# Linear attention in a hybrid decoder step: level products for each head alone, on 64 rows, into two banks

## The chip, the cores and the metric

The kernel runs on one core of one Trainium2 chip. A core has a matrix engine (TensorE, PE in the profile, with its weight loads shown apart as PEld), VectorE (DVE), ScalarE (ACT), GpSimd (POOL) and a queue engine for transfers (SyncE, SP). Operands lie in SBUF, 128 partitions ("rows") wide. TensorE writes its results to PSUM, which has eight banks of 512 fp32 columns. Each engine runs its own instructions in order and waits for others through semaphores.

The metric is device time in microseconds (us) for the whole program. Before the change it is 1334.49 us, the median of three runs (1328.85 to 1334.85).

## The reference, cut to what matters

One layer of a decoder: a norm, one input projection, eight heads of windowed attention beside four heads of gated linear attention, and an output projection. The prompt has 2048 positions, and a sample batch has 64 more. Only the linear attention is touched by the change. Its heads have 64 key columns and 128 value columns. `log_a` is the logarithm of the forget gate, per position and key column:

```python
log_a = jax.nn.log_sigmoid((g_lr @ w_gate_up + b_gate)) / GATE_TAU      # GATE_TAU = 16

def step(state, xs):                     # one chunk of positions
    qc, kc, vc, gc = xs
    b = jnp.cumsum(gc, axis=2)
    diff = b[:, :, :, None, :] - b[:, :, None, :, :]
    decay = jnp.exp(jnp.where(causal[:, :, None], diff, -jnp.inf))
    scores = jnp.einsum('bhtk,bhsk,bhtsk->bhts', qc, kc, decay)
    o = (jnp.einsum('bhts,bhsv->bhtv', scores, vc)
         + jnp.einsum('bhtk,bhkv->bhtv', qc * jnp.exp(b), state))
    b_last = b[:, :, -1]
    state = (jnp.exp(b_last)[..., None] * state
             + jnp.einsum('bhsk,bhsv->bhkv', kc * jnp.exp(b_last[:, :, None] - b), vc))
    return state, o
```

The score of a query `t` and a key `s` needs a decay that depends on both and on the key column, so it isn't one matrix product. It becomes one for a block of queries against a block of keys before them, if both are scaled relative to one position between the blocks: `q_t k_s exp(b_t - b_s) = (q_t exp(b_t - b_m)) (k_s exp(b_m - b_s))`.

## The kernel before

**Levels.** The kernel uses chunks of 128 positions and splits the triangle of a chunk into levels (`LEVELS`, block sizes B = 1, 2, 4, 8, 16, 32, 64). On level B the positions fall into pairs of neighbouring blocks of B. The queries of each second block meet the keys of the first block, both scaled relative to the last position of the first block. The seven levels and the diagonal cover every pair of positions once.

**Units.** `gla_core` treats 256 positions, so two chunks and four heads; there are eight such units for the prompt (tiles named `..._e`). Two heads lie together on the 128 rows: head 2p on rows 0 to 63 and head 2p+1 on rows 64 to 127. So kT, qT and the summed gates b have two halves p of 256 columns. For each level there is a front and a back:

- `front` (lines 229 to 255). GpSimd subtracts the reference position from b (tile `D`, line 236). ScalarE takes exponentials of it into `E` (line 244): one for the keys on all 128 rows, and two for the queries, each on the 64 rows of one head, into two separate layers of `E`. The rest of these two layers is zero from the start. VectorE multiplies keys by layer 0 (`ks`, line 249), and queries by layers 1 and 2 at once (`qbd`, line 252). So `qbd` has the queries twice: once with zeros in place of the second head, once with zeros in place of the first.
- `back` (lines 257 to 292). TensorE multiplies `ks` (128 rows, 64 columns, the stationary operand) with both layers of `qbd`. Because of the zeros, one product over 128 rows gives the scores of each of the two heads. Below B = 64 (line 281) a product has 64 keys and 2 x 32 queries, eight products a level, alternating between output rows 0 to 63 and 64 to 127. VectorE copies the valid ones under a mask into `Ac` (line 287). At B = 64 (line 267) it has 64 keys and 2 x 64 queries, four products a level, and ScalarE copies the result into `full` (line 273). An fp32 product is two instructions on TensorE, each with its weight load.

**PSUM.** The level scores take tiles of the pool `ps_S`, which has two banks in turn: a level's products may start as soon as the copy of the level before last is done. Attention's scores (`qk`, line 436) and the transposes of the mix (line 1611) take tiles of the same pool, at other times.

**What follows.** When all levels of a unit are in, `filled` moves the triangle into `full`, and `chunk` (line 1266) multiplies each head's scores with the values (line 1289), adds the state's part (line 1283), and updates the state `Sbd` (lines 1275 and 1296).

**Order.** `gla_prompt` runs front of level s, then back of level s - 2, then yields; it is woven with the projections (`project`, line 1127, which keep TensorE busy with f16 products `acc_g`, `acc_vb`, `acc_gb`) and with `late_dots` (line 1515 on GpSimd, line 970 on VectorE) by fixed shares. The framework's planner then places instructions on each engine's queue by a simulated timeline, and adds semaphores where a tile, or in PSUM a bank, is written or read by another engine.

Of the kernel before, what the change touches and what calls it, by code (L numbers as in the profile page):

```python
# [7 lines left out]
F32 = mybir.dt.float32  # L8
# [10 lines left out]
P = 128  # L19
# [33 lines left out]
def tile_hymba(ctx: ExitStack, tc: tile.TileContext, A: dict):  # L53
# [86 lines left out]
        DVE.scalar_tensor_tensor(out, a[:n], 1.5, r[:n], ALU.add, ALU.mult)  # L140


    class gla_core:

        def __init__(self, pools, st, row0, n, C, levels, scan_m, mask, tagp, full=None, keep=None):
# [17 lines left out]
        def turn(self):  # L163
# [10 lines left out]
            Ac = self.Ac = keep.tile(  # L174
                [P, nch * 4, 64], F32, name=f"Ac_{tagp}", tag="A", bufs=two
            )
            POOL.tensor_tensor(
                Ac[:C],
                ident64[:C].unsqueeze(1).to_broadcast([C, nch * 4, 64]),
                dd[:C].unsqueeze(2).to_broadcast([C, nch * 4, 64]),  # L180
                ALU.mult,
            )

# [45 lines left out]
        def front(self, li):  # L229
            gt, st, n, B = self.pools[1], self.st, self.n, self.levels[li]  # L230
            halves = lambda f: f.rearrange("p (m two B) -> p m two B", two=2, B=B)
            M = n // B
            bv = halves(self.b[:].rearrange("p a c -> p (a c)"))
            D = gt.tile([P, 2 * n], F32, name=f"D_{self.tagp}_{B}", tag="D", bufs=2)
            dv = halves(D[:])
            dec = POOL.tensor_tensor(  # L236
                dv, bv, bv[:, :, 0:1, B - 1 : B].to_broadcast([P, M, 2, B]), ALU.subtract
            )
            E = st["E"][li % 2]
            ev = E[:, :, :n].rearrange("p i (m B) -> p i m B", B=B)  # L240
            for i, (rows, half) in enumerate(
                ((slice(0, P), 0), (slice(0, 64), 1), (slice(64, P), 1))
            ):
                ACT.activation(  # L244
                    ev[rows, i], dv[rows, :, half, :], AF.Exp, scale=(2 * half - 1) / 16.0
                )
            ks, qbd = st["ks"][li % 3], st["qbd"][li % 3]
            kv, qv = (halves(f.rearrange("p a c -> p (a c)")) for f in (self.kT, self.qT))
            DVE.tensor_tensor(  # L249
                halves(ks[:, : 2 * n])[:, :, 0, :], kv[:, :, 0, :], ev[:, 0], ALU.mult  # L250
            )
            que = DVE.tensor_tensor(  # L252
                qbd[:, :, :n].rearrange("p i (m B) -> p i m B", B=B),
                qv[:, :, 1, :].unsqueeze(1).to_broadcast([P, 2, M, B]), ev[:, 1:3], ALU.mult,
            )
            st["pins"] = (dec.ins, que.ins)

        def back(self, li):
            st, n, C, nch, B = self.st, self.n, self.C, self.nch, self.levels[li]
            ps_s, Ac = self.pools[3], self.Ac  # L260
            ks, qbd = st["ks"][li % 3], st["qbd"][li % 3]
            sc = ps_s.tile([P, 512], F32, name=f"sc_{self.tagp}_{B}", tag="S")
            if B == 64:

                for c in range(nch):
                    for p in range(2):
                        PE.matmul(
                            sc[:64, (c * 2 + p) * P : (c * 2 + p + 1) * P],
                            ks[:, p * n + c * C : p * n + c * C + 64],
                            qbd[:, :, (p * nch + c) * 64 : (p * nch + c + 1) * 64],  # L270
                            start=True, stop=True,
                        )
                ACT.activation(
                    self.full[0:64, :, 64:], sc[:64].rearrange("p (g t) -> p g t", t=64), AF.Copy
                )
                return
            for c in range(nch):
                for p in range(2):
                    o = (c * 2 + p) * 64
                    for k0 in range(0, C, 64):  # L280
                        PE.matmul(
                            sc[k0 : k0 + 64, o : o + 64],
                            ks[:, p * n + c * C + k0 : p * n + c * C + k0 + 64],
                            qbd[:, :, p * (n // 2) + (c * C + k0) // 2 :][:, :, :32],
                            start=True, stop=True,
                        )
            DVE.copy_predicated(
                Ac[:C].rearrange("p g (m two B) -> p g m two B", two=2, B=B)[:, :, :, 1, :],
                self.mask[:C, li].bitcast(I32).unsqueeze(1)
                .to_broadcast([C, nch * 4, 32]).rearrange("p g (m B) -> p g m B", B=B),  # L290
                sc[:C, : nch * 128].rearrange("p (g m B) -> p g m B", g=nch * 4, B=B),
            )

        def queries(self):
# [85 lines left out]


    with ExitStack() as c1:
        ps_Y, ps_S, ps_P, ps_O = (
            c1.enter_context(tc.tile_pool(name=f"ps_{n}", bufs=2, space=PSUM)) for n in "YSPO"
        )
        kp = c1.enter_context(tc.tile_pool(name="p1c", bufs=1))
        sm = c1.enter_context(tc.tile_pool(name="sm", bufs=2))
        wp = c1.enter_context(tc.tile_pool(name="wp", bufs=3))
# [42 lines left out]
        def attend(tag, nh, nb, scores, mask, vf, nmf, denf, OT, pre=None, post=None, neg=-1.0):  # L431
# [4 lines left out]
            t = {}  # L436

            def qk():
                s_ps = ps_S.tile([P, 512], F32, name=f"s_{tag}", tag="S")
                s = t["s"] = sp.tile([P, 512], F32, name=f"p_{tag}", tag="s")  # L440
                for i in range(nh):
                    prods = scores(i)
# [799 lines left out]
                )  # L1242

        Sbd = []
        st = {"wgu": wgu, "E": [], "ks": [], "qbd": []}
        for lst, nm_, shape, m, eng in (
            (st["E"], "E", [P, 3, 256], 2, DVE), (st["ks"], "ks", [P, 512], 3, DVE),
            (st["qbd"], "qbd", [P, 2, 256], 3, DVE), (Sbd, "Sbd", [P, 2, 256], 2, POOL),
        ):
            for i in range(m):  # L1250
                t = gst.tile(shape, F32, name=f"{nm_}{i}")
# [15 lines left out]
        def chunk(core, gc):  # L1267
# [13 lines left out]
            for p in range(2):  # L1281
# [5 lines left out]
                for j in range(2):  # L1287
                    h = 2 * p + j
                    PE.matmul(
                        O[:, h * P : (h + 1) * P], full[:, c * 4 + h, :],  # L1290
                        vb[:, h * P : (h + 1) * P], start=(gc == 0), stop=(gc == 0 or j == 1),
                    )
            for p in range(2):
# [71 lines left out]
        def sample_gla():  # L1365
            while "dots" not in mixed:
# [10 lines left out]
            SP.dma_start(vb[:], vb_d[S : S + NS, :])  # L1377
            own = g1.tile([P, 512], F32, name="own", tag="vx")
            DVE.memset(own[:], 0.0)
            E, ks, qbd = (  # L1380
                own[:, 0:192].rearrange("p (i c) -> p i c", i=3), own[:, 192:320],
                own[:, 320:448].rearrange("p (i c) -> p i c", i=2),
            )
            own = {"wgu": wgu, "E": [E] * 2, "ks": [ks] * 3, "qbd": [qbd] * 3}
            core = gla_core(
                gpools, own, S, NS, NS, LEVELS[:3], scn, masks, "smp", keep=(g1, 1)
            )
# [24 lines left out]
            for p in range(2):  # L1412
                O = ps_O.tile([P, 512], F32, name=f"O_s{p}", tag="O")
                for j in range(2):
# [8 lines left out]
                    for bt in range(8):  # L1423
# [2 lines left out]
                            S0[p][:, bt, :], start=(bt == 0), stop=False,  # L1426
                        )
                    PE.matmul(
                        O[:NS, j * P : (j + 1) * P], Am[:NS, h, :],
                        vb[:, h * P : (h + 1) * P], start=False, stop=True,  # L1430
                    )
                ob = g1.tile([NS, 256], F32, name=f"ob_s{p}", tag="ob")
# [177 lines left out]
        def turned(tag, mt):  # L1610

            mhl = cb.tile([P, 2, KT, P], F16, name=f"mh_{tag}", tag="mh")
            for a in range(2):
                pt = ps_S.tile([P, KT, P], F16, name=f"tm_{tag}_{a}", tag="S")
                for k in range(KT):
                    PE.transpose(pt[:, k, :], mt[:, a, k * P : (k + 1) * P], ident16[:])
                ACT.activation(mhl[:, a], pt[:], AF.Copy)  # L1617
            return mhl[:, 0], mhl[:, 1]

        def sample_parts(mix):  # L1620
# [415 lines left out]
```

## Time and profile before

| | before |
|---|---|
| median of three runs | 1334.49 us (1328.85 to 1334.85) |
| profiled execution | 1337.86 us |
| span of the profile | 1336.1 us |
| mean granted TensorE clock | 0.974 |
| fronts and backs of the prompt | 56 (8 units x 7 levels) |
| first and last start on `E` | 740.6 us, 1007.1 us |

The profile is one execution, taken by the hardware profiler. A row of a group of instructions names line, engine, operation, tiles (out<-in), shapes (partitions x columns) and count, then busy time in us, the mean duration of one in ns, and the idle time of the engine before them with what ended it. For a matmul, `128*64` says that 128 rows and 64 columns of the array are used. Matmuls are pipelined: a duration is the time from start to end of one, while the next one may start long before that. A row of the timeline has start (us from the span's start), duration in us, engine, line and count of merged instructions, and in brackets the engine's idle time ahead of it with what ended it ("issue" is time in which it waited for nothing that the profile shows).

### The profile page before, as it was taken

What the parts mean: (1) busy time and instruction counts of PE and PEld (TensorE: products, weight loads), DVE (VectorE), ACT (ScalarE), POOL (GpSimd) and SP (SyncE); (2) the same over time, 40 slices, a digit from 0 to 9 for tenths busy, and PEclk for the clock granted to TensorE, in tenths of its full rate; (3) what the DMA queues carried; (4) which work ended last, traced back from release to release, by engine and by line L of the source; (5) the groups of instructions that cost most, each with busy time, mean ns of one, the idle gap of its engine ahead of it and who ended that gap; (6) DMA issues with size and microseconds to landing.
All of it is one profiled execution on the core that took longest, in us unless ns stands there. A gap on an engine that the chain in (4) does not pass through costs nothing.

```text
span 1336.1 us, 26268 instructions
## 1 busy us (share of the span) xinstructions
PE 1219.8 (91%) x8910; PEld 732.2 (55%) x8910; DVE 919.4 (69%) x2271; ACT 877.0 (66%) x2332; POOL 631.5 (47%) x596
## 2 busy tenths in 40 slices
PE   3797999989889898998999899999999989999998
PEld 1333565555555555676777566666655445444443
DVE  6357667788767876776765988777672388787741
ACT  5645787777668875878897667665774475565610
POOL 0067545678678745561113965665452144232310
PEclk9989999999999899999899999999999989999999
DMA  8859967777875599969886556553334788998952
GB/s 257 248 152 238 223 198 159 195 209 229 206 201 172 156 265 274 319 218 225 194 210 179 183 165 210 167 167 119 108 101 158 256 253 288 363 344 324 334 194 79
DMA packets 251800, 285.27 MB, mean 214 GB/s; under 512 B 125441, under 2 KB 160338, under 8 KB 251666
## 3 DMA queue, kind: packets, MB, share of 16 engines
q1 hardware_dynamic: 251666, 283.60, 70.7%
q8 instruction: 70, 1.15, 0.4%
q14 instruction: 64, 0.52, 0.1%
HBM read 183.12 MB, written 75.24 MB: 193 GB/s over the span
## 4 chain that ended last, share of the span: by engine, by line
PE 35%; DVE 19%; DMA 16%; issue 11%; ACT 9%; POOL 9%; SPq 2%; POOLq 0%; DVEq 0%; ACTq 0%
PE Y L1658 6%; PE acc_vb L1127 3%; DVE qbd L252 3%; PE acc_gb L1127 3%; PE acc_qkb L1127 3%; PE acc_g L1127 3%; POOL pr L965 2%; PE t L462 2%; PE O L477 2%; DMA T_q<-qp_d 2%; PE s L444 2%; DVE p L452 2%; DVE sck L970 2%; POOL pt L429 2%; DVE ks L249 1%
## 5 line engine op out<-in xcount | busy, mean ns | idle before, releaser
L1127 PEld LDWEIGHTS <-hr 128*128 128x128 f16 x1824 | 174.0, 99 | 133.9 <-issue 16.0
L1127 PEld LDWEIGHTS <-hl 128*128 128x128 f16 x1248 | 122.7, 100 | 154.9 <-issue 28.8
L455 ACT ACTIVATE p<-p,o 128x256 f32<-128x256 f32 (+1 forms) x384 | 173.3, 455 | 47.0 <-DVE o L452 39.8
L1658 PE MATMUL Y<-w_o,mh 128*128 128x512 f16 x768 | 178.0, 383 | 6.7 <-ACT mh L1617 6.6
L965 POOL TENSOR_TENSOR pr<-k,qb 128x512 f32<-128x512 f32 x96 | 132.5, 1380 | 91.8 <-DVE sck L970 58.6
L429 POOL TENSOR_TENSOR pt<-p,pt 128x512 f16<-128x512 f32 (+1 forms) x80 | 94.2, 1178 | 156.3 <-ACT pt L428 125.9
L477 PE MATMUL O<-v,pt 128*128 128x128 f16 x1200 | 113.1, 223 | 22.1 <-POOL pt L429 9.7
L1658 PEld LDWEIGHTS <-mh 128*128 128x128 f16 x768 | 71.9, 98 | 94.3 <-issue 9.0
L970 DVE TENSOR_REDUCE sck<-pr 128x8 f32<-128x512 f32 x128 | 85.6, 678 | 48.9 <-POOL pr L965 48.7
L462 PE MATMUL t<-ident,p 128*128 128x128 f32 x600 | 108.8, 286 | 7.3 <-ACT p L455 5.7
L477 PEld LDWEIGHTS <-pt 128*128 128x128 f16 x1200 | 83.7, 100 | 47.5 <-POOL pt L429 14.3
L1127 PE MATMUL acc_v<-w_v,hl 128*128 128x512 f16 x384 | 96.5, 396 | 8.8 <-DVE vp L759 3.1
L1127 PE MATMUL acc_g<-w_g,hr 128*128 128x272 f16 (+1 forms) x768 | 102.9, 280 | 0.0
L452 DVE CUSTOM_DVE_ANT_0 p<-s,m3w,scl_s 128x128 f32<-128x128 f32 (+1 forms) x256 | 89.0, 394 | 15.9 <-PE s L444 5.7
L1700 POOL TENSOR_TENSOR tc<-oc,w 128x512 f32<-128x512 f32 x32 | 47.0, 1490 | 111.7 <-DVE w L1692 104.8
L1127 PE MATMUL acc_q<-w_q,hl 128*128 128x512 f16 x384 | 93.8, 394 | 4.6 <-ACT zs_k L677 3.8
L244 ACT ACTIVATE E<-D_e 128x256 f32<-128x256 f32 x168 | 66.2, 417 | 43.8 <-POOL D_e L236 26.2
L1127 PE MATMUL acc_k<-w_k,hl 128*128 128x512 f16 x384 | 90.4, 381 | 3.1 <-ACT zs_k L677 2.6
L1127 PE MATMUL acc_vb<-w_vb,hr 128*128 128x512 f16 x384 | 89.1, 379 | 2.3 <-ACT zg L733 2.3
L444 PE MATMUL s<-kk,qq 128*128 128x256 f16 (+1 forms) x512 | 82.4, 273 | 8.9 <-DMA kk<-kp_d 5.2
L1127 PE MATMUL acc_gb<-w_gb,hr 128*128 128x512 f16 x384 | 87.7, 381 | 0.0
L462 PEld LDWEIGHTS t<-ident,p 128*128 128x128 f32 x600 | 70.3, 146 | 18.1 <-ACT p L455 11.3
(509 smaller groups left out, 2630.4 us busy)
## 6 DMA issues: line engine op xcount, KB each, us to landing
k<-in_cache_k_win SPq DMA_DIRECT2D x104, 256.0 KB
sv<-in_cache_v_win SPq DMA_DIRECT2D x24, 1024.0 KB
hr<-h_d SPq DMA_DIRECT2D x44, 512.0 KB
qb<-q_d SPq DMA_DIRECT2D x64, 256.0 KB
o_d<-o SPq DMA_DIRECT2D x96, 132.0 KB
oc<-o_d SPq DMA_DIRECT2D x48, 264.0 KB
x<-in_x_prompt SPq DMA_DIRECT2D x16, 512.0 KB
h_d<-hl SPq DMA_DIRECT2D x16, 512.0 KB
```

The source lines that it names most:

```text
L244: ACT.activation(ev[rows, i], dv[rows, :, half, :], AF.Exp, scale=(2 * half - 1) / 16.0)
L429: POOL.tensor_tensor(l, f, h, ALU.subtract)
L444: PE.matmul(s_ps[:, i * w : (i + 1) * w], q, k, start=(n == 0), stop=(n == len(prods) - 1),)
L452: DVE.tensor_tensor_reduce(s[:, sl], s_ps[:, sl], mask, neg, BIG, ALU.add, ALU.min, nmf(i))
L455: ACT.activation(s[:, sl], s[:, sl], AF.Exp, bias=nmf(i), scale=-1.0, accum_out=denf(i))
L462: PE.transpose(p_ps[:, i * P : (i + 1) * P], t["s"][:, i * P : (i + 1) * P], ident[:])
L477: PE.matmul(o_, t["pt"][:, c, (i * nb + b) * P : (i * nb + b + 1) * P], vf(i, b), start=(n == 0), stop=(n == 2 * nb - 1),)
L965: POOL.tensor_tensor(pr[:], kt, qt, ALU.mult)
L970: DVE.tensor_reduce(out, pr[:].rearrange("p (u k d) -> p u k d", u=2, k=4), AX.X, ALU.add)
L1127: PE.matmul(z, a_[:, k, :], w[:, p_, k, cols], start=(k == 0 and i == 0), stop=(k == KT - 1 and i == 2),)
L1658: PE.matmul(Y[:], a_[:, k, :], w_[:, part, k, :512], start=(i == 0), stop=(i == len(prods) - 1),)
L1700: eng.tensor_tensor(t_[:], oc[:, g, :, 0:64], w[:, g].unsqueeze(2).to_broadcast([P, NH, HD]), ALU.mult,)
```

## The change

The queries of both heads keep their places on the 128 rows: `E` has two layers in place of three, one exponential covers both heads, and `qs` (256 columns) takes the place of `qbd` (two layers of 256). In `back` each product is taken for one head alone, on its 64 rows: twice as many products, each over 64 rows in place of 128 and with half as many columns. The scores of the first head of a pair go into one bank and those of the second head into another, so a level uses both banks of `ps_S`. The pool of two tiles becomes one tile of two banks, `s_pair`, in the class `banks`; attention and the transposes of the mix take its halves in turn (`one`), a level takes it whole (`both`). Heads stand in `Ac` and `full` in the order (head of the pair, chunk, pair).

```diff
+    class banks:
+        def __init__(self, pool):
+            self.pair, self.n = pool.tile([P, 2, 512], F32, name="s_pair"), 0
+        def one(self):
+            self.n += 1
+            return self.pair[:, self.n % 2]
+        def both(self):
+            return self.pair
...
             E = st["E"][li % 2]
             ev = E[:, :, :n].rearrange("p i (m B) -> p i m B", B=B)
-            for i, (rows, half) in enumerate(
-                ((slice(0, P), 0), (slice(0, 64), 1), (slice(64, P), 1))
-            ):
+            for half in range(2):
                 ACT.activation(
-                    ev[rows, i], dv[rows, :, half, :], AF.Exp, scale=(2 * half - 1) / 16.0
-                )
+                    ev[:, half], dv[:, :, half, :], AF.Exp, scale=(2 * half - 1) / 16.0
+                )
...
             que = DVE.tensor_tensor(
-                qbd[:, :, :n].rearrange("p i (m B) -> p i m B", B=B),
-                qv[:, :, 1, :].unsqueeze(1).to_broadcast([P, 2, M, B]), ev[:, 1:3], ALU.mult,
+                qs[:, :n].rearrange("p (m B) -> p m B", B=B), qv[:, :, 1, :], ev[:, 1], ALU.mult
             )
...
-            sc = ps_s.tile([P, 512], F32, name=f"sc_{self.tagp}_{B}", tag="S")
+            sc = ps_s.both()
+            heads = (slice(0, 64), slice(64, P))
             if B == 64:
                 for c in range(nch):
                     for p in range(2):
-                        PE.matmul(
-                            sc[:64, (c * 2 + p) * P : (c * 2 + p + 1) * P],
-                            ks[:, p * n + c * C : p * n + c * C + 64],
-                            qbd[:, :, (p * nch + c) * 64 : (p * nch + c + 1) * 64],
-                            start=True, stop=True,
-                        )
+                        g = c * 2 + p
+                        for j, rows in enumerate(heads):
+                            PE.matmul(
+                                sc[:64, j, g * 64 : g * 64 + 64],
+                                ks[rows, p * n + c * C : p * n + c * C + 64],
+                                qs[rows, (p * nch + c) * 64 : (p * nch + c + 1) * 64],
+                                start=True, stop=True,
+                            )
...
             for c in range(nch):
                 for p in range(2):
-                    o = (c * 2 + p) * 64
+                    o = (c * 2 + p) * (256 // nch)
                     for k0 in range(0, C, 64):
-                        PE.matmul(
-                            sc[k0 : k0 + 64, o : o + 64],
-                            ks[:, p * n + c * C + k0 : p * n + c * C + k0 + 64],
-                            qbd[:, :, p * (n // 2) + (c * C + k0) // 2 :][:, :, :32],
-                            start=True, stop=True,
-                        )
+                        for j, rows in enumerate(heads):
+                            PE.matmul(
+                                sc[k0 : k0 + 64, j, o : o + 32],
+                                ks[rows, p * n + c * C + k0 : p * n + c * C + k0 + 64],
+                                qs[rows, p * (n // 2) + (c * C + k0) // 2 :][:, :32],
+                                start=True, stop=True,
+                            )
             DVE.copy_predicated(
...
-                sc[:C, : nch * 128].rearrange("p (g m B) -> p g m B", g=nch * 4, B=B),
+                sc.rearrange("p j (g f) -> p (j g) f", g=nch * 2)[:C, :, :32].rearrange(
+                    "p g (m B) -> p g m B", B=B
+                ),
             )
...
-        ps_Y, ps_S, ps_P, ps_O = (
-            c1.enter_context(tc.tile_pool(name=f"ps_{n}", bufs=2, space=PSUM)) for n in "YSPO"
+        ps_Y, ps_P, ps_O = (
+            c1.enter_context(tc.tile_pool(name=f"ps_{n}", bufs=2, space=PSUM)) for n in "YPO"
         )
+        ps_S = banks(c1.enter_context(tc.tile_pool(name="ps_S", bufs=1, space=PSUM)))
...
-                s_ps = ps_S.tile([P, 512], F32, name=f"s_{tag}", tag="S")
+                s_ps = ps_S.one()
...
-                        O[:, h * P : (h + 1) * P], full[:, c * 4 + h, :],
+                        O[:, h * P : (h + 1) * P], full[:, 4 * j + 2 * c + p, :],
...
-                pt = ps_S.tile([P, KT, P], F16, name=f"tm_{tag}_{a}", tag="S")
+                pt = ps_S.one().bitcast(F16).rearrange("p (k i) -> p k i", k=KT)
```

Left out: `turn` builds `Ac` in the new order of heads (line 177), the copy at B = 64 reads both banks, and the sample's unit (`own`, one chunk of 64 positions, three levels) has the new tiles in the same way.

## What the change was predicted to do

> **What bounds the kernel now.** I read the page first, then busy time by stretch, since the share of a whole span mixes stages.
>
> ```profile
> span 1336.1 us, 26268 instructions
> PE 1219.8 (91%) x8910; PEld 732.2 (55%) x8910; DVE 919.4 (69%) x2271; ACT 877.0 (66%) x2332; POOL 631.5 (47%) x596
> ```
>
> The change touches the linear-attention stage. The instructions on its tile `E` say when it runs (count, min/median/max ns, first and last start in us):
>
> ```profile
> L249 DVE TENSOR_TENSOR ks<-kq_e,E x56: 394/652/1486, 741.1 to 1006.5; 128x256 f32<-128x256 f32 x56
> L252 DVE TENSOR_TENSOR qbd<-kq_e,E x56: 670/1522/3148, 741.9 to 1007.1; 128x512 f32<-128x512 f32 x56
> ```
>
> So it runs from 741 to 1007 us. Busy time of that stage in stretches of 40 us (columns PE, PEld, DVE, ACT, POOL, granted clock, DMA share, GB/s):
>
> ```profile
> 740.00:780.00 40.00, 34.25 (x338) 24.48 (x336) 38.24 (x48) 26.49 (x70) 36.32 (x29) 0.96 0.57 182
> 780.00:820.00 40.00, 37.05 (x320) 25.49 (x319) 34.77 (x54) 28.21 (x77) 26.52 (x21) 1.00 0.51 155
> 820.00:860.00 40.00, 39.23 (x357) 27.20 (x356) 32.43 (x52) 24.13 (x64) 23.28 (x19) 1.00 0.65 207
> 860.00:900.00 40.00, 39.57 (x358) 27.89 (x357) 28.69 (x43) 25.07 (x65) 26.34 (x22) 1.00 0.53 164
> 900.00:940.00 40.00, 39.24 (x342) 27.45 (x340) 27.62 (x46) 25.69 (x69) 25.57 (x23) 1.00 0.43 120
> ```
>
> Two regimes. From 740 to 820 us VectorE has 38.24 and 34.77 of 40 us, and TensorE has holes (34.25, 37.05). From 820 us on TensorE is full (39.2 to 39.6 of 40) and VectorE and ScalarE have room. There, work taken off VectorE or ScalarE returns nothing unless TensorE was waiting for it. So the second view is what TensorE waits for by name in the whole stage, 740 to 1030 us (us in total, times, longest):
>
> ```profile
> PE U L1275 <- DVE Sbd L1296: 3.7, 5, 1.2
> PE sc_e L281 <- DVE qbd L252: 2.7, 3, 1.4
> PE mx_o L582 <- DVE mm_o L581: 2.6, 1, 2.6
> PE acc_vb L1127 <- ACT zg L733: 2.3, 1, 2.3
> PE sc_e L267 <- DVE Ac_e L287: 2.1, 1, 2.1
> PE O L1283 <- ACT ob_c L330: 0.5, 1, 0.5
> PE sc_e L281 <- DVE Ac_e L287: 0.4, 1, 0.4
> ```
>
> All of it is 14.3 us. The rows that hang on VectorE's queue in linear attention (`Sbd`, `qbd`, twice `Ac_e`) are 3.7 + 2.7 + 2.1 + 0.4 = **8.9 us**: the most that a lighter VectorE can return.
>
> **The change part by part.** These groups are touched (count, busy us, mean ns, then idle time before them):
>
> ```profile
> L252 DVE TENSOR_TENSOR qbd<-kq_e,E 128x512 f32<-128x512 f32 x56 | 71.1, 1269 | 0.5 <-ACT E L244 0.4
> L244 ACT ACTIVATE E<-D_e 64x256 f32<-64x256 f32 x112 | 46.5, 416 | 8.9 <-DVE qbd L252 7.3
> L249 DVE TENSOR_TENSOR ks<-kq_e,E 128x256 f32<-128x256 f32 x56 | 40.7, 727 | 17.6 <-ACT E L244 9.8 <-PE sc_e L281 5.9 <-PE acc_g L1127 1.6
> L281 PE MATMUL sc_e<-qbd,ks 128*64 128x64 f32 x768 | 35.3, 229 | 3.1 <-DVE qbd L252 2.7 <-DVE Ac_e L287 0.4
> L287 DVE COPY_PREDICATED Ac_e<-gmask,sc_e 128x256 f32<-128x256 int32 x48 | 25.4, 530 | 17.3 <-PE sc_e L281 16.8
> L267 PE MATMUL sc_e<-qbd,ks 128*64 128x128 f32 x64 | 9.4, 293 | 2.1 <-DVE Ac_e L287 2.1
> ```
>
> *ScalarE.* Two exponentials on 64 rows become one on 128 rows: 56 fronts lose one of 416 ns, 23.3 us. ScalarE is busy for at most 28 of 40 us in each stretch, so this alone pays nothing; it shortens a front by 0.4 us.
>
> *VectorE.* The query product shrinks from 512 to 256 columns, the shape of `ks` beside it. By the minima of the first two rows it saves 670 - 394 = 276 ns, by the means of the groups 1269 - 727 = 542 ns: 15.5 to 30.4 us over 56. The gap between minimum and median (670 against 1522 ns) is time spent held, not streaming. The Trainium skill (SBUF — State Buffer, "Who interferes with whom") says that a VectorE instruction with two SBUF inputs is held while GpSimd reads SBUF; the spread agrees, and by that rule the hold stays and 15.5 us is nearer. For TensorE either saving is worth between 0 and the 8.9 us above. I take half, **-4.5 us**: POOL, also near full from 740 to 780 us (36.32 of 40), is late next there, while the waits for `Sbd` end with a queue of VectorE work that gets shorter by some 0.5 us for each front in it.
>
> *TensorE, levels below 64.* A level was 16 instructions (8 fp32 products, two each) with 64 columns streamed; it becomes 32, on 64 rows, with 32 columns. One level and the last level of the second pair of chunks:
>
> ```profile
> 789.55 0.68 PE L281 MATMUL sc_e<-qbd,ks 128*64 128x64 f32 x16
> ...
> 791.90 1.09 PE L267 MATMUL sc_e<-qbd,ks 128*64 128x128 f32 x8
> ```
>
> The last instruction's own time is latency (means of the groups: 229 and 293 ns), so the starts spread over 0.68 - 0.23 = 0.45 us, 30 ns each, and 1.09 - 0.29 = 0.80 us, 114 ns each. Twice the columns cost nearly four times as much, because `L281` alternates between two column halves of the array (output rows 0 to 63 and 64 to 127), which run together, and `L267` uses one half: some 60 ns per instruction and half at 64 columns. After the change there are four quarters with 8 instructions each. Streaming 32 columns would let each take 30 ns; its weights set the floor:
>
> ```profile
> L1428 PEld LDWEIGHTS O_s<-vb_s,Ac_smp x8: 129/130/133, 999.8 to 1018.4; 64*64 64x64 f32 x8
> ```
> ```profile
> 999.80 0.19 PEld L1428 LDWEIGHTS O_s<-vb_s,Ac_smp 64*64 64x64 f32 x2 [0.17 <-issue]
> ```
>
> Two weight loads of the new 64x64 shape take 0.19 us, one 0.13, so they start 0.06 us apart. A level thus takes 8 x 0.06 = 0.48 us if all four quarters run together: no change, **0**. No row shows two row halves together. The bounds are 0.24 us (streaming alone) and 16 x 0.06 = 0.96 us (two at a time): -0.21 to +0.51 us, times 48 levels -10 to +24 us. I take 0, since it is what the weight row gives with the concurrency that the column halves show. The idle time ahead of this shape, 0.17 us, is no longer than ahead of a level now (0.21 us in the row at 812.47 us, below), so switching shapes costs the same.
>
> The instruction count could bind instead. In this trace 16 products on four column quarters start within 0.43 - 0.23 = 0.20 us, 13 ns apart, so it need not:
>
> ```profile
> 1104.97 0.43 PE L1821 MATMUL R<-ksT,qx 128*32 128x64 f32 x16
> ```
>
> The Trainium skill (TensorE: Matmul & The Clock Gate, "Wait — 56ns, not 53.3ns?") says that matmuls never start closer than some 25 ns apart; by that, 32 take 0.8 us, an estimated +17 us over 48 levels. The 13 ns of the row disagree.
>
> *TensorE, level 64.* 8 instructions with 128 columns on one half become 16 with 64 columns on two row halves: 8 x 0.06 = 0.48 us in place of 0.80 + 0.06 = 0.86. That is -0.38 us, times 8, **-3.0 us** of a full TensorE; +0.1 us each, +0.8 in all, if the halves don't run together.
>
> *Both banks at once.* A level's scores now fill both banks of `s_pair`, so the next level's first matmul waits for the copy of the level before; until now two levels had a bank each. Behind that matmul stand `sc_e`, the projections (`acc_g`, `acc_vb`) and the state products in TensorE's order, and VectorE's next copy waits for them. Where VectorE is late, TensorE did run ahead:
>
> ```profile
> 746.14 0.69 PE L281 MATMUL sc_e<-qbd,ks 128*64 128x64 f32 x16 [0.89 <-DVE qbd L252]
> ```
> ```profile
> 749.10 0.72 DVE L287 COPY_PREDICATED Ac_e<-gmask,sc_e 128x256 f32<-128x256 int32 x1
> ```
>
> The first row is the second level; its predecessor's copy ended only at 749.10 + 0.72, 3.7 us after that start. The longest lead comes while VectorE splits the weights of `gb`:
>
> ```profile
> 812.47 0.55 PEld L281 LDWEIGHTS sc_e<-qbd,ks 128*64 128x64 f32 x16 [0.21 <-issue]
> ```
> ```profile
> 819.61 0.73 DVE L287 COPY_PREDICATED Ac_e<-gmask,sc_e 128x256 f32<-128x256 int32 x1
> ```
>
> Here it is 819.61 + 0.73 - 812.47 = 7.9 us. These don't add up: once TensorE is a level later it stays so, and the planner, which knows the dependence, can put projections ahead. Bounds 0 and +7.9 us. I take **+2**, nearer to the lower end, because the same lag swallows waits that follow it (2.1 us at `L267`, some of the 2.7 us for `qbd`).
>
> *At nothing.* The masked copy reads eight runs with a stride, and `Ac` is built in another order: same elements, under TensorE from 820 us on; if their cover went, a copy could cost the 727 - 530 = 0.2 us that parts it from `ks`, or save as much. Attention and the transposes of the mix take the two banks in turn as the pool did. The sample's three levels have 4 instructions each before.
>
> **Sum**: -4.5 + 0 - 3.0 + 2 = **-5.5 us**. The profiled execution took 1337.86 us (span 1336.1), giving 1332.4; it stands 3.4 us above the median of 1334.49, which gives **1329.0 us**. The bounds of relief and of the bank wait alone: -11.9 (all 8.9, no bank wait) to +4.9 (no relief, all 7.9), 1322.6 to 1339.4.
>
> **The rivals.**
> 1. *The four quarters run only two at a time* (slower). Place: `back`. Price: 0.96 - 0.45 = 0.51 us x 48 = +24.5, level 64 +0.8, relief and bank wait -2.5: +22.8 us, 1357. It turns slower than before once a level takes 0.11 us (5.5/48) more than now. For it: no row shows row halves together. Against it: column halves and quarters do run together. The same price follows if starts can't come closer than the 30 ns of `L281`, whatever the tiles; the 13 ns row speaks against that. Chance 0.10, 0.02 of it for the floor on starts. (The floor of the Trainium skill's page on TensorE, above, is this second form.)
> 2. *No change.* The waits move to the next late thing on VectorE or POOL and the bank wait takes the 3.0 us of level 64: 1334. For it: 39 of 40 us busy on TensorE. Chance 0.33.
> 3. *The chain is right.* The chain that ended last has DVE 19% and `qbd` 3%:
>
> ```profile
> PE 35%; DVE 19%; DMA 16%; issue 11%; ACT 9%; POOL 9%; SPq 2%; POOLq 0%; DVEq 0%; ACTq 0%
> PE Y L1658 6%; PE acc_vb L1127 3%; DVE qbd L252 3%; PE acc_gb L1127 3%; PE acc_qkb L1127 3%; PE acc_g L1127 3%; POOL pr L965 2%; PE t L462 2%; PE O L477 2%; DMA T_q<-qp_d 2%; PE s L444 2%; DVE p L452 2%; DVE sck L970 2%; POOL pt L429 2%; DVE ks L249 1%
> ```
>
> 3% is 40 us; 43% less (542/1269) is -17, with level 64 -20: 1314.5. Against it: where TensorE is full, a chain through VectorE runs beside it. Chance 0.10.
> 4. *The bank wait in full*: -3.0 - 2 + 7.9 = +2.9, 1337.4. Chance 0.07.
>
> **How the numbers follow.** Forecast 0.40, rivals 0.10, 0.33, 0.10, 0.07. A measurement tells about 0.5%, 6.7 us, from no change. Faster by more: 0.26 of the forecast's share, rival 3 and a little of 2, 0.38. Slower by more: rival 1 and the tails of 4, 0.16. Within: 0.46. The range 1316 to 1342 leaves out rival 1 and part of 3.
>
> **What would show it.** Right: `E` x112, a product `qs` of 256 columns near 0.7 us, 32 matmuls of 64*64 per level within 0.5 us of starts, level 64 within 0.5 us, fewer waits for `Sbd`. Wrong: levels of 0.7 us and more; waits of the level products for `Ac_e` of several us between 744 and 825 us; or another order by the planner in attention, before 735 us, where nothing should move.

## The result: 7.4% slower, and where the time sits

The changed kernel takes **1432.26 us** (median of four runs, 1431.13 to 1433.92), the kernel before 1334.67 us (1328.85 to 1346.16) beside it. The ratio is **1.0741**, 95% interval 1.0708 to 1.0773. The forecast was 1329.0 us with a range of 1316 to 1342.

The page of the changed kernel, span and busy time:

```profile
span 1431.9 us, 27986 instructions
PE 1264.2 (88%) x9754; PEld 741.6 (52%) x9754; DVE 901.3 (63%) x2271; ACT 855.4 (60%) x2273; POOL 612.4 (43%) x596
```

VectorE and ScalarE have less to do than before (901.3 against 919.4, 855.4 against 877.0 us), as the change intends. TensorE is 88% busy, hardly less than 91%. That share misleads: it says nothing of a loss of 96 us.

The level products, on which the forecast spent most of its words, do what it said. In the timeline of the changed kernel, the last level and a lower one:

```profile
906.24 0.68 PE L280 MATMUL s_pair<-qs,ks 64*64 64x64 f32 x16
...
912.12 0.67 PE L296 MATMUL s_pair<-qs,ks 64*64 64x32 f32 x32
```

From the groups of instructions, one row a group:

```profile
L263 DVE TENSOR_TENSOR qs<-kq_e,E 128x256 f32<-128x256 f32 x56 | 41.8, 746 | 0.0
...
L296 PE MATMUL s_pair<-qs,ks 64*64 64x32 f32 x1536 | 32.6, 222 | 3.4 <-DVE Ac_e L302 2.3 <-DVE qs L263 1.2
```

The 32 instructions start within 0.67 - 0.22 = 0.45 us, as the 16 did, and the last level within 0.46 in place of 0.80 us. TensorE's idle time ahead of the lower levels adds up to 3.4 us. So the loss isn't there. The last product of attention and the first exponential of linear attention tell where it is; rows of the tiles `O` and `E`, kernel before and then changed kernel:

```profile
L477 PE MATMUL O<-v,pt x1200: 216/220/315, 157.7 to 729.0; 128*128 128x128 f16 x172
```
```profile
L495 PE MATMUL O<-v,pt x1200: 216/219/314, 154.7 to 812.1; 128*128 128x128 f16 x172
...
L255 ACT ACTIVATE E<-D_e x112: 399/417/447, 836.0 to 1115.1; 128x256 f32<-128x256 f32 x112
```

Attention, which the change was not meant to touch, ends at 812.1 in place of 729.0 us: **83 of the 96 us of span are lost before linear attention begins.** Linear attention begins 23.9 us after that, where it was 740.6 - 729.0 = 11.6 us.

TensorE's waits by name over attention (us in total, times, longest), before and then changed:

```profile
PE s L444 <- DVE o L452: 8.6, 8, 4.0
```
```profile
PE s_pair L462 <- DVE o L470: 27.1, 33, 3.3
```

The scores of attention wait for VectorE to read scores (`o` is a column that the same instruction leaves), three times as long and four times as often. The timeline shows which scores. Before, eight products (two tiles of scores) run ahead, and VectorE reads them behind:

```profile
517.62 0.49 PE L444 MATMUL s<-kk,qq 128*128 128x256 f16 x3
...
518.79 0.27 PE L444 MATMUL s<-kk,qq 128*128 128x256 f16 x1
...
519.79 0.60 PE L444 MATMUL s<-kk,qq 128*128 128x256 f16 x4
...
520.54 0.48 DVE L452 CUSTOM_DVE_ANT_0 p<-s,m3c,scl_s 128x256 f32<-128x256 f32 x1
```

After the change, the next four products come only after both reads of the four before, although they go to the other bank:

```profile
560.30 0.60 PE L462 MATMUL s_pair<-kk,qq 128*128 128x256 f16 x4
...
563.77 0.48 DVE L470 CUSTOM_DVE_ANT_0 p<-s_pair,m3c,scl_s 128x256 f32<-128x256 f32 x1
...
564.17 0.48 DVE L470 CUSTOM_DVE_ANT_0 p<-s_pair,m3c,scl_s 128x256 f32<-128x256 f32 x1
...
565.94 0.60 PE L462 MATMUL s_pair<-kk,qq 128*128 128x256 f16 x4
```

In between TensorE runs 20 products of a projection (`acc_qkb`). It is the same over all of attention: counted in the two traces from the start of a score's first product to the end of its reading, more than 512 score columns are under way for 252 us before (1024 at most), and never after. So the framework keeps order tile by tile here, and not bank by bank as the description of the kernel before has it for PSUM, and the two halves of `s_pair` are one tile (the run two_tiles, below, tests it).

What pays is the work that filled TensorE. Busy time by stretch (PE, PEld, DVE, ACT, POOL, clock, DMA share, GB/s), before and then changed:

```profile
350.00:450.00 100.00, 88.75 (x635) 55.93 (x633) 75.22 (x185) 71.93 (x204) 76.21 (x68) 0.96 0.73 199
...
650.00:750.00 100.00, 94.36 (x877) 71.41 (x876) 64.04 (x229) 81.22 (x283) 31.15 (x30) 1.00 0.79 212
```
```profile
350.00:450.00 100.00, 76.48 (x550) 49.72 (x549) 76.73 (x192) 70.03 (x202) 69.93 (x66) 0.90 0.75 189
...
650.00:750.00 100.00, 80.55 (x737) 62.48 (x736) 67.24 (x261) 82.83 (x294) 17.35 (x15) 0.91 0.59 144
```

Products per 100 us fall from 635 to 550 and from 877 to 737 (the last 20 us of the latter stretch were linear attention's before). The projections beside attention are used up early, since they are what can run while a score waits:

```profile
L1127 PE MATMUL acc_v<-w_v,hl x384: 376/379/635, 25.7 to 426.7; 128*128 128x512 f16 x192
```
```profile
L1145 PE MATMUL acc_v<-w_v,hl x384: 376/379/634, 25.8 to 367.7; 128*128 128x512 f16 x192
```

They end 59 us earlier, and from 385 to 513 us attention has hardly any product of a projection beside it, where before that was so from 444 to 465 us. The holes also explain most of the busy share. TensorE is busy for 1264.2 - 1219.8 = 44.4 us *more*, with no more columns to stream, since the row counts the latency of the last product ahead of each hole. Its busy time falls into 229 unbroken stretches in place of 110, and the ends of these stretches, from the start of the last product on, add up to 66.7 in place of 30.8 us, which is 35.9 of the 44.4.

### The profile page after: what moved, and what is told of

It reads as the page before. It is cut to its first block, busy times and chain, and to the rows that moved or that the text cites. A ratio compares the mean times of both kernels' runs of the same rounds, so it can differ in the third digit from the quotient of the medians.

```text
span 1431.9 us, 27986 instructions
## 1 busy us (share of the span) xinstructions
PE 1264.2 (88%) x9754; PEld 741.6 (52%) x9754; DVE 901.3 (63%) x2271; ACT 855.4 (60%) x2273; POOL 612.4 (43%) x596
## 5 line engine op out<-in xcount | busy, mean ns | idle before, releaser
L983 POOL TENSOR_TENSOR pr<-k,qb 128x512 f32<-128x512 f32 x96 | 126.9, 1321 | 90.7 <-DVE sck L988 51.4
L495 PE MATMUL O<-v,pt 128*128 128x128 f16 x1200 | 120.3, 230 | 25.7 <-DVE o L512 10.6
L480 PE MATMUL t<-ident,p 128*128 128x128 f32 x600 | 123.1, 297 | 17.3 <-ACT p L473 14.3
L495 PEld LDWEIGHTS <-pt 128*128 128x128 f16 x1200 | 88.0, 103 | 54.9 <-POOL pt L447 10.3
L470 DVE CUSTOM_DVE_ANT_0 p<-s_pair,m3w,scl_s 128x128 f32<-128x128 f32 (+1 forms) x256 | 89.6, 396 | 30.5 <-PE s_pair L462 17.8
L462 PE MATMUL s_pair<-kk,qq 128*128 128x256 f16 (+1 forms) x512 | 78.7, 279 | 24.0 <-DVE o L470 19.1
L1717 POOL TENSOR_TENSOR tc<-oc,w 128x512 f32<-128x512 f32 x32 | 42.6, 1350 | 129.1 <-DVE w L1709 127.4
L249 POOL TENSOR_TENSOR D_e<-b_e 128x512 f32<-128x512 f32 x56 | 61.6, 1103 | 78.8 <-ACT E L255 62.7
```

The source lines that it names most:

```text
L249: dec = POOL.tensor_tensor(dv, bv, bv[:, :, 0:1, B - 1 : B].to_broadcast([P, M, 2, B]), ALU.subtract)
L462: PE.matmul(s_ps[:, i * w : (i + 1) * w], q, k, start=(n == 0), stop=(n == len(prods) - 1),)
L470: DVE.tensor_tensor_reduce(s[:, sl], s_ps[:, sl], mask, neg, BIG, ALU.add, ALU.min, nmf(i))
L480: PE.transpose(p_ps[:, i * P : (i + 1) * P], t["s"][:, i * P : (i + 1) * P], ident[:])
L495: PE.matmul(o_, t["pt"][:, c, (i * nb + b) * P : (i * nb + b + 1) * P], vf(i, b), start=(n == 0), stop=(n == 2 * nb - 1),)
L983: POOL.tensor_tensor(pr[:], kt, qt, ALU.mult)
```

## The experiments

Two theories at first. **Theory 1**: one tile for two banks in attention is the whole loss. **Theory 2**: linear attention pays by itself, since its stage came out longer (from the first `E` to the last level it is 740.6 to 1022.2 us before and 836.0 to 1131.8 after, 281.6 and 295.8 us, so 14.2 us; the expectations below take it as 298 and 16). **Theory 3**, on where buffers lie, came from the first four runs. All times are medians; ratios are to the kernel before on the same chip, with their 95% interval.

| run | us | ratio (interval) |
|---|---|---|
| pair_linear_only | 1351.4 | 1.0142 (1.0104 to 1.0180) |
| pair_old_products | 1429.3 | a single run |
| two_tiles | 1341.0 | 1.0046 (1.0024 to 1.0069) |
| old_one_bank | 1339.5 | 1.0037 (1.0017 to 1.0056) |
| pair_linear_padded | 1324.9 | 0.9924 (0.9899 to 0.9950) |
| two_tiles_padded | 1331.1 | 0.9975 (0.9957 to 0.9994) |
| old_shifted | 1340.1 | 1.0051 (1.0019 to 1.0083) |
| products_alone | 1333.4 | 1.0001 (0.9979 to 1.0022) |
| pair_small_pad | 1321.4 | 0.9906 (0.9886 to 0.9926) |
| changed_padded | 1428.3 | 1.0716 (1.0684 to 1.0748) |
| pair_two_sets | 1348.1 | 1.0106 (1.0085 to 1.0128) |
| pair_linear_gap | 1340.4 | 1.0053 (1.0029 to 1.0077) |
| pair_attention_linear | 1418.1 | 1.0619 (1.0574 to 1.0664) |

### The tile of two banks

**pair_linear_only**: the changed kernel, the pair in linear attention only.

```diff
-        ps_S = banks(c1.enter_context(tc.tile_pool(name="ps_S", bufs=1, space=PSUM)))
...
+        ps_S = c_att.enter_context(tc.tile_pool(name="ps_S", bufs=2, space=PSUM))
...
-        gpools = (gl, gt, ps_O, ps_S, ps_P)
+        gpools = (
+            gl, gt, ps_O,
+            banks(c_gla.enter_context(
+                tc.tile_pool(name="ps_G", bufs=1, space=PSUM, reuse_waits="tile"))),
+            ps_P,
+        )
...
+        ps_S = c1.enter_context(tc.tile_pool(name="ps_S2", bufs=2, space=PSUM, reuse_waits="tile"))
...
```

> The changed kernel, but the tile of two banks exists only in linear attention; attention's scores and the transposes of the mix again take two tiles of one bank each from a pool of two. Theory 1 (the whole loss is attention's: its two score banks are halves of one tile, and a write to one half waits for the reading of the other): the loss of 98 us is gone and the sum of the prediction holds, 1329 us, 1322 to 1337; attention's last O product ends near 717 us as before. Theory 2 (linear attention pays by itself, since its stage took 298 us in place of 282): the 16 us stay, 1346 to 1352. Under both no more than 512 score columns... of attention are limited, that is, up to 1024 are in flight again.

Measured 1351.4 us, with attention's last product at 727 us, much as before (729.0; the 717 of the expectation is a slip). 81 us are gone, so attention is the larger part; the rest lies in the range of theory 2 (1346 to 1352).

**pair_old_products**: the kernel before with the class `banks`; attention, transposes and the level scores call `one()`, everything else is old.

> The kernel before with nothing but the pool replaced: attention, the transposes and the level scores take halves of one tile of two banks in turn; the products over 128 rows with zero blocks, three exponentials and one bank per level are as before. Theory 1: slow without any of the new products, 1420 to 1440 us, most of it ahead of the first exponential of linear attention (near 830 us in place of 741). Theory 2: at most 1420, since the 16 us of linear attention belong to the new products. If the loss needs the new products: 1335.

A single run, 1429.3 us, with none of the new products. Attention ends late:

```profile
L490 PE MATMUL O<-v,pt x1200: 216/219/314, 156.8 to 810.4; 128*128 128x128 f16 x172
```

This settles the larger part: it needs the tile alone.

**two_tiles**: the changed kernel, with two tiles of one bank behind the same class.

```diff
-            self.pair, self.n = pool.tile([P, 2, 512], F32, name="s_pair"), 0
+            self.pair = [pool.tile([P, 512], F32, name=f"s_pair{i}") for i in range(2)]
+            self.n = 0
...
-            return self.pair[:, self.n % 2]
+            return self.pair[self.n % 2][:]
...
```

> The changed kernel, but the pair is two tiles of one bank each, taken in turn by attention and the transposes, and both by a level, whose copy is split into two instructions, one for each bank. Theory 1: no wait from one half to the other, so 1329 us and some 3 us for the 56 more copies, 1325 to 1340. Rival (the place of the banks or the fixed alternation in place of a pool costs, not that it is one tile): it stays at 1420 to 1432.

1341.0 us: same alternation of two banks, but two tiles, and attention is whole again. Its last product and TensorE's wait for the reading of scores (9.2 us in 10 times up to 720 us, where the changed kernel had 27.1 in 33):

```profile
L500 PE MATMUL O<-v,pt x1200: 216/219/314, 156.1 to 725.1; 128*128 128x128 f16 x172
```
```profile
PE s_pair L467 <- DVE o L475: 9.2, 10, 3.7
```

The time stands just above the range of theory 1 (1325 to 1340), so something is left.

**old_one_bank**: the kernel before, its level scores in a pool of one bank, so each level waits for the copy of the level before; attention and the transposes get pools of their own, with two banks.

> The kernel before with the old products, but the scores of all levels go to one bank, so that each level waits for the copy of the level before; attention keeps its two banks. This is the wait for both banks by itself. The prediction's step: +2 us, bounds 0 and +7.9, 1335 to 1343. Theory 2 by this wait: about +16 us, 1351. Theory 1 has the 16 us from projections left over from attention, so it agrees with the first figure.

1339.5 us, +4.9 us (0.0037 x 1334.5; 2.3 to 7.5). The wait exists and is small; it isn't theory 2's 16 us. What the pools cut by stage do by themselves is in this number and wasn't measured apart.

### Where buffers lie

In pair_linear_only linear attention begins late. Rows of the first unit's load `zqk_e` (first and last start), kernel before, then pair_linear_only:

```profile
L155 SPq DMA_DIRECT2D zqk_e<-zqk_d x8: 370/382/608, 600.7 to 894.0; - x8
```
```profile
L167 SPq DMA_DIRECT2D zqk_e<-zqk_d x8: 371/401/560, 729.7 to 881.8; - x8
...
L255 ACT ACTIVATE E<-D_e x112: 398/417/449, 746.9 to 1020.5; 128x256 f32<-128x256 f32 x112
```

The load starts 129 us later, only when attention is over. `E` and `qs` are smaller: 2 x 1024 + 3 x 1024 = 5120 bytes a partition. Whatever is allocated behind them moves down by that much, and by the built program's list of buffers (not printed here; the times of the loads agree) the first `zqk_e` comes to lie over attention's outputs `o`, which are in use to the end, where it lay over keys. In old_one_bank, with the old sizes, the load is at 599.0 us. **Theory 3**: this placement is what theory 2 took for the products' cost.

**pair_linear_padded**: pair_linear_only with unused columns behind each `E` and `qs`.

```diff
                 lst.append(t)
+                if nm_ in ("E", "qs"):
+                    gst.tile([P, 256], F32, name=f"{nm_}x{i}")
```

> The pair in linear attention only (1351.4 us), with unused columns behind each E and qs, so that all later buffers lie where they lay before the change. In the traces so far the first load of a unit (zqk_e) starts at 600.7 us before the change and at 729.7 us with the smaller E and qs, since its buffer then lies over attention's last outputs (tile o) and not over its keys. Theory 3 (this placement delays the first front by some 8 us, and the end with it): the transfer starts near 600 us again, the first exponential near 739 us in place of 746.9, and the time is 1341 to 1345. Theory 2 (the 16 us are the level products' and their wait): it stays at 1348 to 1352.

```profile
L255 ACT ACTIVATE E<-D_e x112: 398/417/459, 738.5 to 1001.6; 128x256 f32<-128x256 f32 x112
...
L167 SPq DMA_DIRECT2D zqk_e<-zqk_d x8: 371/377/463, 598.4 to 886.3; - x8
```

1324.9 us. The load is early again, and the gain of 26.5 us is three times what the 8 us of `E` explain. Theory 2 falls; theory 3 has the cause and not the size. The kernel is now **faster than before, 0.9924**.

**two_tiles_padded**: two_tiles with the same columns.

> Two tiles of one bank (1341.0 us) with the same unused columns. Theory 3: 1341 less 8 to 9 us, 1332 to 1334, first exponential near 737 us. Theory 2: 1341, unchanged. If the terms of the prediction hold beside the placement (VectorE relief 4.5, level 64 3.0, bank wait 2): 1329.

1331.1 us, 9.9 us faster than two_tiles: theory and size agree here, the size in part by luck, since the columns also end a second cost that pair_linear_gap, below, finds (`rv_ob` starts 21.6 us behind the last product of linear attention in two_tiles and 2.0 us here). It is 6 us slower than one pair with one copy a level (1324.9); that it has two copies a level is the likely reason, not a tested one.

**old_shifted**: the kernel before, only `Sbd` allocated elsewhere (`gc` in place of `gst`).

> The kernel before, old products and all, with only the two state buffers Sbd allocated behind the other buffers, so that the first unit's zqk_e lies over attention's last outputs, as after the change. Theory 3: the first zqk_e transfer moves from 600.7 us to about 729 us, the first exponential from 740.6 to 748, and the time to 1340 to 1344. If the delay is swallowed later: 1335.

1340.1 us, 0.0051 x 1334.5 = +6.8 us (2.5 to 11.1), load at 734.4 us, first `E` at 751.5 us. An old kernel with not one changed instruction loses half a per cent by the place of two buffers.

**pair_small_pad**: pair_linear_only with one unused stretch of 2304 bytes behind `E`, `ks`, `qs` and `Sbd`.

> The pair in linear attention only, E and qs in their small sizes side by side, and 576 unused columns (2304 bytes) once behind them: the least that moves the first unit's load buffer off attention's last outputs, while the other buffers lie elsewhere than before the change. If the load alone makes the difference between 1351.4 and 1324.9 us: first zqk_e transfer near 600 us and a time of 1322 to 1330. If it was the place of other buffers: above 1333.

1321.4 us, load at 591.7 us. Its interval overlaps that of pair_linear_padded; the best kernel of the study, 0.9906.

**pair_linear_gap**: what makes 26.5 us of 8? In pair_linear_only the output stage's preparation (`rv_ob`, the square root for the norm) stands behind the sample's last state update in VectorE's queue:

```profile
1079.46 0.69 DVE L1489 TENSOR_TENSOR S<-S,U_s 128x512 f32<-128x512 f32 x1 [3.15 <-PE U_s L1478]
1080.06 0.21 DVE L1580 TENSOR_SCALAR va<-pw_v 128x1 f32<-128x1 f32 x2
1080.19 0.83 DVE L122 TENSOR_SCALAR rv_ob<-ob_ss 128x68 f32<-128x68 f32 x1
```

The last product of linear attention was over at 1059.6 us. By the built programs' lists of buffers (not printed here), the last of the output stage (`obl_s`) shares 32 bytes with the first of the sample (`scan_s`) in this kernel, in two_tiles and in the changed one, and in no other; these are the kernels in whose traces `rv_ob` is late (pair_small_pad has it 2.0 us behind the last product, so it does not part the two costs). A gap behind the tables of linear attention ends that and leaves the load late (728.3 us):

```diff
+        gc.tile([P, 64], F32, name="space")
```

> The pair in linear attention only, small E and qs (1351.4 us), with 64 unused columns behind the tables of linear attention and nothing else: the sample's buffers move up by 256 bytes, so that the output stage's last buffer (obl_s) no longer shares 32 bytes with the sample's first (scan_s). The first load stays late (zqk_e near 730 us). In the traces so far the output stage's rv_ob runs 2 to 5 us after the last product of linear attention wherever these two don't share bytes, and 13 to 22 us after it where they do. If that late preparation is the larger part of the 26.5 us: 1333 to 1338, rv_ob within 5 us of the last O. If the late load is all of it: 1348 to 1352.

```profile
1063.06 0.20 DVE L122 TENSOR_SCALAR rv_ob<-ob_ss 128x68 f32<-128x68 f32 x1 [0.21 <-ACT obq_c L351]
...
1066.44 0.69 DVE L1490 TENSOR_TENSOR S<-S,U_s 128x512 f32<-128x512 f32 x1 [1.76 <-PE U_s L1479]
```

`rv_ob` is ahead again, 4 us behind the last product. 1340.4 us lies between the two cases of the expectation: 11.0 us of the 26.5 are this overlap, and 15.5 us go with the late load. The late load alone cost the old kernel 6.8 us (old_shifted). Why a first front 7 us late (745.4 against 738.5 us) costs 15.5 us stays open: from first front to last product, linear attention takes 1059.1 - 745.4 = 313.7 us here and 1040.7 - 738.5 = 302.2 us in pair_linear_padded, and TensorE's waits by name in that stage hold 5 of these 11.5 us (15.4 against 10.2 us; for `Sbd` 8.3 against 2.3).

### The parts of the change, and the ledger

**products_alone**: the new products with the old fronts; each product reads its head's layer of `qbd`.

```diff
-                                qs[rows, p * (n // 2) + (c * C + k0) // 2 :][:, :32],
+                                qs[rows, j, p * (n // 2) + (c * C + k0) // 2 :][:, :32],
...
```

> The pair in linear attention only, products on 64 rows into two banks, but the fronts as before: three exponentials, qbd in two layers, of which each product reads the layer of its head (so E and qbd have their old sizes and the placement is as before). Against pair_linear_padded it shows what the lighter front returns by itself. By the prediction's relief it is 4.5 us slower than that run (bounds 0 and 8.9); if VectorE's relief returns nothing, the same within 2 us. Against old_one_bank (1339.5 us), which has the same wait with old products, it shows the products: 3.0 us faster by the prediction.

Ratio 1.0001. With old_one_bank (1.0037) and pair_linear_padded (0.9924): the products return 0.0036 x 1334.5 = 4.8 us (give or take 3.9, from the two intervals), the lighter front 0.0077 x 1334.5 = 10.3 us (give or take 4.4). The planner orders each of these kernels anew, and no run holds its order fixed, so how much of a term of a few us is the order's stays open.

**changed_padded**: the changed kernel with the unused columns only.

> The changed kernel itself, with the unused columns behind each E and qs and nothing else. It leaves attention's one tile as the only known loss. If the losses add (placement 26.5 from 1351.4 against 1324.9): 1406. If placement is worth only what it is worth in the kernel before or with two tiles (5.9, 9.9): 1422 to 1426. If attention's late end hides it: 1432.

1428.3 us, 3.9 us less than the changed kernel, and the intervals overlap. With attention late, the two placements hardly matter; their cost does not add.

**pair_attention_linear**: pair_linear_padded, attention on halves of one tile.

> pair_linear_padded (1324.9 us), but attention takes halves of one tile again; only the transposes of the mix keep a pool of two. Against changed_padded (1428.3 us) it shows what one tile costs in the output stage, against pair_linear_padded what it costs in attention. Attention's last O product ended at 809.9 us in changed_padded and at 727.1 in pair_linear_padded, so attention alone is some 83 us: 1408. The output stage lasted 251 and 242 us: some 9 us. If attention is all of the 103.4 us: 1428.

1418.1 us: attention's share is 1418.1 - 1324.9 = 93.2 us, the transposes' 1428.3 - 1418.1 = 10.2 us (give or take 7, from the two intervals). First to last product of the output stage, pair_attention_linear and then changed_padded:

```profile
L1684 PE MATMUL Y<-w_o,mh x768: 379/379/634, 1169.8 to 1412.7; 128*128 128x512 f16 x192
```
```profile
L1677 PE MATMUL Y<-w_o,mh x768: 376/379/634, 1168.1 to 1419.0; 128*128 128x512 f16 x192
```

243 against 251 us. Of the 93.2 us, attention itself has 813.0 - 726.8 = 86.2.

**pair_two_sets**: pair_linear_padded with two pairs of banks for the levels, the gate transposes moved to the banks of the state products.

> pair_linear_padded (1324.9 us) with two pairs of banks for the level scores in turn, so that a level waits for the copy of the level before last as before the change; the two further banks come from the gate transposes, which take banks of the state products' pool in linear attention. The wait for both banks was +4.9 us with old products: if that is what is left, 1320. Rival: the state products and transposes, now on two banks together, wait for one another, 1325 or more.

1348.1 us, slower by 23 us, on the rival's side. The cause isn't shown: TensorE's largest waits by name are for `Ac_e` (6.7 us at the lower levels, 5.2 in pair_linear_padded) and for `Sbd` (6.0 against 2.3 us). So the run doesn't price the wait for both banks.

The ledger, each term the difference of two medians, so that they add up by construction: 1334.7 before; the change in linear attention alone -9.8; attention on one tile +93.2; transposes on one tile +10.2; placement beside these +3.9; 1432.3 after.

## Why the prediction was wrong, point by point

**The step that failed** is the sentence under *At nothing*: "Attention and the transposes of the mix take the two banks in turn as the pool did." They take them in turn, but not as the pool did. A pool of two hands out two tiles; two halves of one tile are one buffer for the framework, and every tile of scores waits for the reading of the one before. That sentence stood for 103.4 us. The sign that would show it was named ("another order by the planner in attention, before 735 us, where nothing should move"), but as the planner's doing and not as a wait, and it was given no price, no rival and no chance. The trace of before had it: attention's scores on TensorE and their reading on VectorE overlap by a whole tile there (517.62 to 520.54 us above), and a change of their buffer should have been priced by that.

**A second step was absent**: that smaller tiles move all buffers behind them. Worth 26.5 us without the first loss and 3.9 us beside it.

**What held**, with the kernel free of both (pair_linear_padded, 0.9924, a gain of 10.1 us with 6.7 to 13.5 as interval):

- *Levels below 64, 0*: 0.45 us before and after. The four quarters run together; rival 1 is out. By the Trainium skill (TensorE: Matmul & The Clock Gate, "Wait — 56ns, not 53.3ns?") starts are never nearer than some 25 ns; 32 instructions in 0.45 us are 14 ns apart, so the runs disagree here too.
- *Level 64, -3.0 us*: 0.46 in place of 0.80 us of starts is -0.34 a level, -2.7 in all. The products as a whole returned 4.8, give or take 3.9.
- *Both banks at once, +2 us*: +4.9 us, inside the bounds of 0 and 7.9, nearer to their middle.
- *VectorE, -4.5 us*: 10.3 us, give or take 4.4, for the lighter front as a whole (the shorter product and one exponential less). Half of the 8.9 us of named waits was too little; the whole of it was nearer. What VectorE itself saves was at the lower of the two ends (15.5 and 30.4). `qbd` took 1269 ns in the mean before and `qs` takes 746 after, but that difference isn't the size alone: with the old 512 columns the mean is 1049 in products_alone and 1034 in pair_old_products, and with 256 columns it is 813 in pair_linear_padded and 746 in the changed kernel. Like for like that is 236 and 288 ns, 13.2 and 16.1 us over 56. The Trainium skill's rule (SBUF — State Buffer, "Who interferes with whom") was read as leaving the held time in place, which spoke for 15.5, and the runs agree: 22 and 23 of the 56 products take over 0.9 us in products_alone and pair_linear_padded, each of them beside an instruction of GpSimd. Their rows:

```profile
L265 DVE TENSOR_TENSOR qs<-kq_e,E 128x512 f32<-128x512 f32 x56 | 58.8, 1049 | 1.9 <-ACT E L257 1.8
```
```profile
L263 DVE TENSOR_TENSOR qs<-kq_e,E 128x256 f32<-128x256 f32 x56 | 45.5, 813 | 0.0
```

- The sum of these, -5.5 us, was right in sign and too small by some 5, with errors that pull against each other (5.8 us too little for the front and 1.8 us for the products, against 2.9 us too little for the bank wait): the interval of pair_linear_padded is 1321.0 to 1327.8 us (0.9899 and 0.9950 of 1334.5), and 1329.0 was forecast.

The other rivals are outside of that interval too: no change (1334), the chain (1314.5), the bank wait in full (1337.4).

## What to carry to other kernels

A buffer that is merged, cut or shared changes who waits for whom at every place that uses it: ask of each user, also those that the change isn't about, how far the writer runs ahead of the reader, and price that lead. A tile that shrinks moves everything allocated behind it; before reading a loss as the cost of new instructions, see whether the first loads of the next stage still start when they did, and pad to the old size as a test. And a busy share that hardly falls is no sign of health: compare counts of instructions per stretch.

## What the runs showed of the hardware

Products on two halves of the array's rows ran together: 16 of 64x64 with 64 columns each started within 0.46 us, where 8 of 128x64 with 128 columns took 0.80 us. So did products on four quarters (two halves of rows by two halves of columns): 32 with 32 columns started within 0.45 us, where 16 on two column halves with 64 columns took as long. The granted clock was 0.90 and 0.91 in the two stretches of attention shown above, with TensorE busy for 76.48 and 80.55 of 100 us, and 0.96 and 1.00 in the same stretches before, with 88.75 and 94.36. What of the loss that makes was not measured by itself.
